# Block-by-block merge, output projection and second norm in a diffusion layer kernel, with gates fetched a channel tile ahead

## The chip, the cores and the metric

The kernel runs on one core of one Trainium2 chip. The time is device microseconds from start to end of one execution. In the text PE is TensorE, DVE is VectorE, ACT is ScalarE, POOL is GpSimd and SP is SyncE, whose queue issues every DMA of this kernel. "PEld" is the loading of weights into PE, which overlaps the matmuls.

## The reference

2048 latent positions of 1024 channels (and 256 context tokens) pass through a mixer and a gated convolutional MLP. The part that matters here lies between the two:

```python
def merge_branches(u, y_hgrn, w_a, w_b, w_out):
    y_a = fourier_mix(u[..., OFF_FNET:OFF_FNET + FNET_DIM]) @ w_a
    y_b = y_hgrn @ w_b
    g_a = jax.nn.sigmoid(u[..., OFF_GA:OFF_GB])
    g_b = jax.nn.sigmoid(u[..., OFF_GB:IN_DIM])
    return (g_a * y_a + g_b * y_b) @ w_out
...
x = x + mx[:, :, 2] * yx
h2 = modulate(rmsnorm(x, norm2_g[layer]), mx[:, :, 3], mx[:, :, 4])
x = x + mx[:, :, 5] * conv_ffn(h2, ...)
return rmsnorm(x, final_g)
```

Two branch outputs of 512 channels each are projected to 1024, multiplied by sigmoid gates and added, projected once more, added to x, and normed and modulated for the MLP.

## The kernel before

Every large product is made of three fp32r matmuls: each operand is split into a high part (ACT casts it, line 102) and a low part (raw minus high, line 103, on POOL or DVE), and hi·hi, hi·lo and lo·hi are added up in PSUM (`mm3`, lines 144 to 146). So every operand that comes from memory takes a DMA, a cast and a subtraction before PE can use it (`load_split`, line 105). The staging tile `rw` between the DMA and the subtraction has two buffers.

The program has three stages. `phase1` computes the input projections, the Fourier branch and the recurrence. Its last projections are the gates GA and GB: PE fills a PSUM bank, ACT evicts it into an `ev` tile of the pool `pe` (line 479), and SP stores that to memory (line 482). `phase2` is the stage of the change. `phase3` and `down` are the MLP.

`phase2` works on four blocks of 512 positions. For a block n there are three pieces of work:

- The merge (`branches`, line 855). Eight tiles `y`, four per branch, are loaded and split once. Then, for each of eight channel tiles j, a pair of weight tiles from w_a and w_b is loaded and split, PE makes 24 matmuls into two `pj` banks, DVE multiplies each by its gate tile (line 879), adds the two (line 881), and the sum is split into `mh` and `ml`. The two gate tiles are fetched in the same turn of the loop (line 876), into buffers of the pool `pe` that `phase1` used for evictions; there are three of them.
- The output projection (`out_proj`, line 886). For each of two halves c of the 1024 columns, 96 matmuls fill four banks, `wo`, under the tags `at` and `o` (two banks each). DVE multiplies them by `m2` and adds them to x (lines 912 and 913). The sums are stored to `dX` for the end of the layer (line 915).
- The second norm (`h2_block`, line 917). ACT sums the squares of the four x tiles (line 923), DVE computes the reciprocal root in a dozen tiny steps and scales x (line 928). The rest is a generator of eight steps (`modulate_steps`, line 419): four PE transposes into one bank (line 426), then an affine step on DVE (line 428), another on ACT (line 429) and a subtraction (line 431). These steps are called one at a time inside the loops of the next block, by `next(bg, None)`.

The order of the blocks before: merge 0, projection 0, merge 1 (with the steps of block 0), projection 1, merge 2 (with the steps of block 1), merge 3, projection 2, projection 3 (with the steps of block 2), and the steps of block 3 in the first matmuls of the MLP (`z`). A scheduler orders the instructions of each engine when the program is built; a pool's tile can only be filled when the tile that had its place has been read for the last time. Pools lie on a stack: `p4`, the pool of `phase2`, lies above `pe` while that one is open. The eight large places H0 to H7 are shared by tag: merges put `ml` and `mh` in H6 and H7, or in H4 and H5 for the last block.

Of the kernel before, what the change touches and what calls it, by code (L numbers as in the profile page):

```python
# [17 lines left out]
F32 = mybir.dt.float32  # L18
F32R = mybir.dt.float32r
# [7 lines left out]
P = 128  # L27
D = 1024
SEQ = 2048
CTX = 256  # L30
NB = 4
TB = 512
# [62 lines left out]
class Layer:  # L95
# [54 lines left out]
    def run(self):  # L150
        tc, nc = self.tc, self.nc
        with ExitStack() as es:
# [11 lines left out]
            with tc.tile_pool(name="pe", bufs=1, reuse_waits="tile") as self.pe:  # L164
                self.phase1()
                self.phase2()
# [252 lines left out]
    def modulate_steps(self, pool, xs, A, B, hi, lo, tags, every):  # L419

        nc = self.nc
        n = len(xs)
        for k in range(KD):
            pt = self.ps.tile([P, TB], F32, name="pt", tag=tags[k % len(tags)])
            for i in range(n):
                nc.tensor.transpose(pt[:, i * P:(i + 1) * P], xs[i][:, k * P:(k + 1) * P], self.eye)
            tmp = pool.tile([P, TB], F32, name="mt", tag="mt", bufs=2)
            nc.vector.tensor_scalar(tmp[:, :n * P], pt[:, :n * P], A[:, k:k + 1], B[:, k:k + 1], op0=MUL, op1=ADD)
            nc.scalar.activation(hi[:, k, :], pt[:, :n * P], AF.Identity, scale=A[:, k:k + 1], bias=B[:, k:k + 1])
            eng = nc.vector if k % every == every - 1 else nc.gpsimd  # L430
            eng.tensor_tensor(lo[:, k, :], tmp[:, :n * P], hi[:, k, :], op=SUB)
            yield
# [398 lines left out]
    def phase2(self):  # L831
        tc, nc, a, ps = self.tc, self.nc, self.a, self.ps
        self.h2 = [[None, None] for _ in range(NB)]
        with tc.tile_pool(name="p4", bufs=1, reuse_waits="tile") as p4:
            mg, bg = {}, iter(())
            for n in (0, 1):
                mg[n] = self.branches(p4, n, "H6", "H7", bg)
                x1 = self.ph.tile([P, 4, D], F32, name=f"x1{n}", tag=f"H{4 + n}")
                xs = [x1[:, i, :] for i in range(4)]
                self.out_proj(p4, n, mg[n], xs, bg)  # L840
                bg = self.h2_block(p4, n, xs, (2 * n, 2 * n + 1), ("tp", "at", "o"))
            mg[2] = self.branches(p4, 2, "H6", "H7", bg)
            mg[3] = self.branches(p4, 3, "H4", "H5", bg)
            for n in (2, 3):
                xs = [p4.tile([P, D], F32, name=f"x1{n}{i}", tag="yo", bufs=10) for i in range(4)]
                self.out_proj(p4, n, mg[n], xs, bg)
# [4 lines left out]
                bg = self.h2_block(p4, n, xs, ((6, 7), (4, 5))[n - 2], ("tp", "pj"))  # L851
# [3 lines left out]
    def branches(self, p4, n, t_lo, t_hi, bg):  # L855

        nc, a, ps = self.nc, self.a, self.ps
        mg_lo = self.ph.tile([P, KD, TB], F32R, name=f"ml{n}", tag=t_lo)
        mg_hi = self.ph.tile([P, KD, TB], F32R, name=f"mh{n}", tag=t_hi)
        br = []  # L860
        for b in range(2):
            for k in range(4):
                y = p4.tile([P, 2, TB], F32R, name=f"y{n}{b}{k}", tag="yo", bufs=10)
                self.load_split(y[:, 0, :], y[:, 1, :],
                                self.dY[k][:, n * TB:(n + 1) * TB] if b == 0 else self.dO[k][n][:], nc.vector, p4)
                br.append((y[:, 0, :], y[:, 1, :]))
        for j in range(KD):
# [5 lines left out]
            gts = []  # L873
            for b in range(2):
                gt = self.pe.tile([P, TB], F32, name="gt", tag="ev", bufs=3)
                nc.sync.dma_start(gt, (self.dGA if b == 0 else self.dGB)[j][n])
# [3 lines left out]
                gts.append(gt)  # L880
            nc.vector.tensor_tensor(gts[0], gts[0], gts[1], op=ADD)
            self.split(mg_hi[:, j, :], mg_lo[:, j, :], gts[0], nc.vector)
            next(bg, None)
        return mg_hi, mg_lo

    def out_proj(self, p4, n, mg, xs, bg):
# [6 lines left out]
        for c in range(2):  # L893
# [3 lines left out]
            accs = [ps.tile([P, TB], F32, name=f"wo{i}", tag="at" if i < 2 else "o") for i in range(4)]  # L897
            for k in range(KD):
# [10 lines left out]
                next(bg, None)  # L909
# [7 lines left out]
    def h2_block(self, p4, n, xs, slots, tags):  # L917
# [8 lines left out]
        rs = self.rsqrt(p4, vv, 4)  # L926
        for i in range(4):
            nc.vector.tensor_scalar(xs[i], xs[i], rs[:, i:i + 1], None, op0=MUL)
        self.h2[n] = [self.ph.tile([P, KD, TB], F32R, name=f"h2{n}{i}", tag=f"H{slots[i]}") for i in range(2)]
        return self.modulate_steps(p4, xs, self.mod2_A, self.mod2_B, *self.h2[n], tags, 4)  # L930
# [160 lines left out]
```

## Time and profile before

| what | value |
|---|---|
| time, median of 3 runs | 3182.1 us (3172.17 to 3186.12) |
| the profiled execution itself | 3175.0 us |
| its span, first to last instruction | 3173.2 us |
| matmuls and transposes on PE | 14955 |
| DVE busy | 1735.2 us |
| ACT busy | 930.4 us |
| POOL busy | 947.3 us |
| bytes moved | 372.59 MB |

The span is what the page's shares refer to; 1.8 us lie around it. PE's busy time counts overlapping matmuls once. "idle before" in the lists of groups is the time in which the engine did nothing just before an instruction of that group, with the instruction that ended the wait.

### The profile page before, as it was taken

How to read it: one execution, taken by the hardware profiler on the slowest of the kernel's cores; microseconds unless marked ns; L12 is line 12 of the kernel's file. 1: busy time of each engine (PE TensorE's matmuls, PEld its weight loads, DVE VectorE, ACT ScalarE, POOL GpSimd, SP SyncE). 2: the span in 40 equal slices, each digit the busy share in tenths (PEclk: the TensorE clock that was granted, in tenths of full speed). 3: DMA queues.
4: the chain of work that ended last, by engine and by line, in shares of the span. 5: the costliest groups of instructions: out<-in, count | busy, mean ns of one | idle time of the engine just before them, and what ended most of it. 6: DMA issues, size and time to landing. Idle time of an engine off the chain costs nothing.

```text
span 3173.2 us, 38929 instructions
## 1 busy us (share of the span) xinstructions
PE 3086.0 (97%) x14955; PEld 2554.0 (80%) x14955; DVE 1735.2 (55%) x2489; ACT 930.4 (29%) x1498; POOL 947.3 (30%) x563
## 2 busy tenths in 40 slices
PE   7999999999999999999999999999999998999998
PEld 4977788888888888777777888888888887788886
DVE  5355534566666640356645777777777777111324
ACT  4322211233333331233333232222222223223322
POOL 2200110000000010343532443444443445444443
PEclk9999999999999999999999999999999999999999
DMA  6255645423223322655642111111111113535643
GB/s 236 80 169 175 194 153 162 141 95 115 93 91 108 106 93 84 212 167 173 193 162 70 60 50 47 53 50 51 53 34 53 53 47 105 183 125 176 205 146 133
DMA packets 278506, 372.59 MB, mean 117 GB/s; under 512 B 20253, under 2 KB 154289, under 8 KB 274993
## 3 DMA queue, kind: packets, MB, share of 16 engines
q1 hardware_dynamic: 278321, 370.11, 35.6%
q8 instruction: 118, 1.93, 0.2%
q14 instruction: 67, 0.55, 0.1%
HBM read 268.58 MB, written 101.45 MB: 117 GB/s over the span
## 4 chain that ended last, share of the span: by engine, by line
PE 77%; DMA 6%; DVE 5%; POOL 2%; issue 2%; ACT 2%; SPq 0%; DVEq 0%; ACTq 0%; POOLq 0%
PE z L146 9%; PE z L145 9%; PE z L144 9%; PE pj L146 8%; PE pj L144 8%; PE pj L145 8%; PE dn L1035 5%; PE dn L1033 5%; PE dn L1034 5%; PE pa L773 4%; DMA rw<-in_w_b_dram 1%; PE kv L645 1%; PE wo L906 1%; PE wo L908 1%; PE wo L907 1%
## 5 line engine op out<-in xcount | busy, mean ns | idle before, releaser
L983 DVE SCALAR_TENSOR_TENSOR ac<-z,cw,ac 128x1953 f32<-128x1953 f32 (+2 forms) x308 | 700.8, 2275 | 255.4 <-ACT be L955 244.1
L144 PE MATMUL z<-h,w_up 128*128 128x512 f32 x1408 | 548.0, 389 | 1.9 <-ACT w_up L102 1.9
L146 PE MATMUL z<-h,w_up 128*128 128x512 f32 x1408 | 548.0, 389 | 0.0
L145 PE MATMUL z<-h,w_up 128*128 128x512 f32 x1408 | 548.0, 389 | 0.0
L959 POOL TENSOR_TENSOR ac<-ac,be 128x1984 f32<-128x1984 f32 x44 | 196.7, 4471 | 427.6 <-DVE ac L983 427.6
L103 POOL TENSOR_TENSOR gl<-rw,gh 128x512 fp32r<-128x512 f32 x176 | 233.0, 1326 | 271.7 <-ACT gh L102 262.2
L144 PEld LDWEIGHTS z<-h,w_up 128*128 128x128 f32 x1408 | 264.4, 188 | 57.0 <-ACT w_up L102 2.3
L145 PEld LDWEIGHTS z<-h,w_up 128*128 128x128 f32 x1408 | 264.4, 188 | 54.8
L146 PEld LDWEIGHTS z<-h,w_up 128*128 128x128 f32 x1408 | 264.4, 188 | 54.5
L1033 PE MATMUL dn<-wd,gh 128*128 128x512 f32 x704 | 279.0, 396 | 6.1 <-ACT gh L102 6.1
L1035 PE MATMUL dn<-wd,gl 128*128 128x512 f32 x704 | 279.2, 397 | 5.6 <-POOL gl L103 5.5
L1034 PE MATMUL dn<-wd,gh 128*128 128x512 f32 x704 | 278.6, 396 | 0.0
L953 ACT ACTIVATE ac<-z,vt,cw 128x2048 f32<-128x2048 f32 x44 | 90.9, 2066 | 639.0 <-PE z L146 639.0
L102 ACT CAST gh<-rw 128x512 fp32r<-128x512 f32 x176 | 108.6, 619 | 308.6 <-PE dn L1034 219.4
L479 ACT ACTIVATE ev<-pj 128x512 f32<-128x512 f32 (+1 forms) x136 | 79.6, 586 | 358.3 <-PE pj L146 336.9
L1035 PEld LDWEIGHTS dn<-wd,gl 128*128 128x128 f32 x704 | 133.3, 189 | 39.1 <-POOL gl L103 8.5
L1033 PEld LDWEIGHTS dn<-wd,gh 128*128 128x128 f32 x704 | 133.4, 189 | 37.6 <-ACT gh L102 7.0
L1051 DVE TENSOR_TENSOR dtmp<-dn,m 128x512 f32<-128x512 f32 x32 | 21.4, 684 | 251.6 <-PE dn L1035 251.5
L1034 PEld LDWEIGHTS dn<-wd,gh 128*128 128x128 f32 x704 | 133.3, 189 | 30.6
L103 POOL TENSOR_TENSOR w_up<-rw,w_up 128x512 fp32r<-128x512 f32 x88 | 112.8, 1306 | 92.0 <-ACT w_up L102 92.0
L773 PEld LDWEIGHTS pa<-bQ,bkc 128*128 128x128 f32 x896 | 120.7, 191 | 17.0 <-issue 10.5
L773 PE MATMUL pa<-bQ,bkc 128*128 128x128 f32 x896 | 127.5, 286 | 1.3
(304 smaller groups left out, 6185.6 us busy)
## 6 DMA issues: line engine op xcount, KB each, us to landing
rw<-dZ SPq DMA_DIRECT2D x176, 256.0 KB, 3.0
rw<-in_ffn_up_dram SPq DMA_DIRECT2D x88, 256.0 KB, 3.4
dZ<-ac SPq DMA_DIRECT2D x22, 1024.0 KB, 4.4
rw<-in_w_in_dram SPq DMA_DIRECT2D x80, 256.0 KB, 3.1
maw<-in_ada_w_dram SPq DMA_DIRECT2D x64, 256.0 KB, 3.1
rw<-in_w_out_dram SPq DMA_DIRECT2D x64, 256.0 KB, 2.6
x<-dX SPq DMA_DIRECT2D x48, 256.0 KB, 5.1
rw<-in_ffn_down_dram SPq DMA_DIRECT2D x44, 256.0 KB, 3.1
```

The source lines that it names most:

```text
L102: self.nc.scalar.copy(hi, raw)
L103: (eng or self.nc.gpsimd).tensor_tensor(lo, raw, hi, op=SUB)
L144: self.nc.tensor.matmul(ps, lh, rh, start=start and i == 0, stop=False)
L145: self.nc.tensor.matmul(ps, lh, rl, start=False, stop=False)
L146: mm = self.nc.tensor.matmul(ps, ll, rh, start=False, stop=stop and i == last)
L773: mm = nc.tensor.matmul(pa[:, c], kc[:, c], fap(Q, w * P, [(2 * m, nw), (W + m, 2), (1, m)]), start=True, stop=True)
L953: nc.scalar.activation(ac, z, AF.Identity, scale=self.cw[:, 4, jj:jj + 1], bias=self.v("cb", jj))
L959: nc.gpsimd.tensor_tensor(ac[:, :SEQ - 64], ac[:, :SEQ - 64], be[:, 64:], op=ADD)
L983: nc.vector.scalar_tensor_tensor(o, z3[:, r0 + dy:r1 + dy, c0 + dx:c1 + dx], self.cw[:, k, jj:jj + 1], o, op0=MUL, op1=ADD)
L1033: nc.tensor.matmul(accs[i], gh[:, t], wh, start=(kk == 0), stop=False)
L1034: nc.tensor.matmul(accs[i], gh[:, t], wl, start=False, stop=False)
L1035: nc.tensor.matmul(accs[i], gl[:, t], wh, start=False, stop=(kk == NF - 1))
```

## The change

The four blocks now go one after the other: merge n, projection n, second norm n, for n from 0 to 3. A merge fetches the gates of channel tile j + 1 before it works on tile j, from four buffers of its own in `p4`; the pool `pe` is closed before `phase2` opens `p4`, so that `p4` lies where `pe` lay. The `y` tiles have 8 places and not 10. The second column half of a projection uses the banks `pj` and `tp`; the first keeps `at` and `o`. The norm steps of a block are called from the second channel tile of the next merge on, with one more at that merge's end, and none inside a projection. Block 2's x goes where block 0's was (H4), which merge 3 needs for `ml`; so block 2's steps read x back from `dX`, four small pieces for each step (`reload_steps`), and scale them there.

```diff
@@ run
             with tc.tile_pool(name="pe", bufs=1, reuse_waits="tile") as self.pe:
                 self.phase1()
-                self.phase2()
+            self.phase2()
...
@@ modulate_steps
-    def modulate_steps(self, pool, xs, A, B, hi, lo, tags, every):
+    def modulate_steps(self, pool, xs, A, B, hi, lo, tags, every, k0=0, nk=KD):
...
-        for k in range(KD):
+        for k in range(k0, k0 + nk):
...
-                nc.tensor.transpose(pt[:, i * P:(i + 1) * P], xs[i][:, k * P:(k + 1) * P], self.eye)
+                nc.tensor.transpose(pt[:, i * P:(i + 1) * P], xs[i][:, (k - k0) * P:(k - k0 + 1) * P], self.eye)
...
@@ phase2
-            mg, bg = {}, iter(())
-            for n in (0, 1):
-                mg[n] = self.branches(p4, n, "H6", "H7", bg)
-                x1 = self.ph.tile([P, 4, D], F32, name=f"x1{n}", tag=f"H{4 + n}")
-                xs = [x1[:, i, :] for i in range(4)]
-                self.out_proj(p4, n, mg[n], xs, bg)
-                bg = self.h2_block(p4, n, xs, (2 * n, 2 * n + 1), ("tp", "at", "o"))
-            mg[2] = self.branches(p4, 2, "H6", "H7", bg)
-            mg[3] = self.branches(p4, 3, "H4", "H5", bg)
-            for n in (2, 3):
-                xs = [p4.tile([P, D], F32, name=f"x1{n}{i}", tag="yo", bufs=10) for i in range(4)]
-                self.out_proj(p4, n, mg[n], xs, bg)
+            bg = iter(())
+            for n in range(NB):
+                mg = self.branches(p4, n, *(("H6", "H7") if n < 3 else ("H4", "H5")), bg)
+                if n < 3:
+                    x1 = self.ph.tile([P, 4, D], F32, name=f"x1{n}", tag=f"H{4 + n % 2}")
+                    xs = [x1[:, i, :] for i in range(4)]
+                else:
+                    xs = [p4.tile([P, D], F32, name=f"x1{n}{i}", tag="yo", bufs=8) for i in range(4)]
+                self.out_proj(p4, n, mg, xs)
                 if n == 3:
...
-                bg = self.h2_block(p4, n, xs, ((6, 7), (4, 5))[n - 2], ("tp", "pj"))
+                bg = self.h2_block(p4, n, xs, ((0, 1), (2, 3), (6, 7), (4, 5))[n], ("tp", "at", "o") if n < 3 else ("tp", "pj"))
...
@@ branches
-        br = []
+        br, gates = [], {}
+
+        def load_gates(j):
+            gates[j] = [p4.tile([P, TB], F32, name=f"gt{b}", tag="gt", bufs=4) for b in range(2)]
+            for b in range(2):
+                nc.sync.dma_start(gates[j][b], (self.dGA if b == 0 else self.dGB)[j][n])
+
...
-                y = p4.tile([P, 2, TB], F32R, name=f"y{n}{b}{k}", tag="yo", bufs=10)
+                y = p4.tile([P, 2, TB], F32R, name=f"y{n}{b}{k}", tag="yo", bufs=8)
...
+        load_gates(0)
         for j in range(KD):
...
-            gts = []
+            if j + 1 < KD:
+                load_gates(j + 1)
+            gts = gates.pop(j)
             for b in range(2):
-                gt = self.pe.tile([P, TB], F32, name="gt", tag="ev", bufs=3)
-                nc.sync.dma_start(gt, (self.dGA if b == 0 else self.dGB)[j][n])
+                gt = gts[b]
...
-                gts.append(gt)
             nc.vector.tensor_tensor(gts[0], gts[0], gts[1], op=ADD)
             self.split(mg_hi[:, j, :], mg_lo[:, j, :], gts[0], nc.vector)
-            next(bg, None)
+            if j:
+                next(bg, None)
+        next(bg, None)
         return mg_hi, mg_lo
...
@@ out_proj
-            accs = [ps.tile([P, TB], F32, name=f"wo{i}", tag="at" if i < 2 else "o") for i in range(4)]
+            accs = [ps.tile([P, TB], F32, name=f"wo{i}", tag=("at", "at", "o", "o")[i] if c == 0 else ("pj", "pj", "tp", "tp")[i])
+                    for i in range(4)]
...
-                next(bg, None)
...
@@ h2_block
         rs = self.rsqrt(p4, vv, 4)
+        hi, lo = self.h2[n] = [self.ph.tile([P, KD, TB], F32R, name=f"h2{n}{i}", tag=f"H{slots[i]}") for i in range(2)]
+        if n == 2:
+            return self.reload_steps(p4, rs, hi, lo, tags)
         for i in range(4):
             nc.vector.tensor_scalar(xs[i], xs[i], rs[:, i:i + 1], None, op0=MUL)
-        self.h2[n] = [self.ph.tile([P, KD, TB], F32R, name=f"h2{n}{i}", tag=f"H{slots[i]}") for i in range(2)]
-        return self.modulate_steps(p4, xs, self.mod2_A, self.mod2_B, *self.h2[n], tags, 4)
+        return self.modulate_steps(p4, xs, self.mod2_A, self.mod2_B, hi, lo, tags, 4)
+
+    def reload_steps(self, p4, rs, hi, lo, tags):
+
+        nc = self.nc
+        for k in range(KD):
+            xc = p4.tile([P, 4, P], F32, name="xc", tag="xc", bufs=2)
+            for i in range(4):
+                nc.sync.dma_start(xc[:, i, :], self.dX[8 + i][:, k * P:(k + 1) * P])
+            nc.vector.tensor_tensor(xc, xc, fap(rs, 0, [(1, 4), (0, P)]), op=MUL)
+            xs = [xc[:, i, :] for i in range(4)]
+            yield from self.modulate_steps(p4, xs, self.mod2_A, self.mod2_B, hi, lo, tags, 4, k, 1)
```

The first place where the order moves is the start of the merges, on the queue of SP. Before, the loads of block 0's `y` (from `dY` and `dO`) stand among the stores of an earlier gate projection:

```order
L482 DMA dGA_0_191<-ev 128x512
L114 DMA rw<-dY_235 128x512
L114 DMA rw<-dY_236 128x512
L896 DMA m_11381<-dm_314 128x512
L114 DMA rw<-dY_237 128x512
L482 DMA dGA_1_192<-ev 128x512
L114 DMA rw<-dY_238 128x512
L114 DMA rw<-dO_0_239 128x512
L114 DMA rw<-dO_0_243 128x512
L482 DMA dGA_2_193<-ev 128x512
L114 DMA rw<-dO_0_247 128x512
L114 DMA rw<-dO_0_251 128x512
```

Now they stand behind the store of the last gate tile:

```order
L483 DMA dGB_3_234<-ev 128x512
L114 DMA rw<-in_w_a_dram 128x4x128
L114 DMA rw<-in_w_b_dram 128x4x128
L901 DMA x_11377<-in_x_dram 128x1024
L114 DMA rw<-dY_235 128x512
L114 DMA rw<-dY_236 128x512
L864 DMA gt_11025<-dGA_0_171 128x512
L864 DMA gt_11026<-dGB_0_203 128x512
L864 DMA gt_11038<-dGA_0_175 128x512
L114 DMA rw<-dY_237 128x512
L114 DMA rw<-dY_238 128x512
L864 DMA gt_11039<-dGB_0_207 128x512
```

Twenty-three more stores of gate tiles now stand ahead of the first load of `y` (in a name such as dGB_3_234 the 3 is the block and the last number a running one), and the loads of the first gates and of x stand between the loads of `y`.

On PE, at the same place, the matmuls of the first channel tile (weights `wab_11029`) all stood ahead of those of the second; now the second's (`wab_11073`) are put between them:

```order
L146 MATMUL pj_11042<-y003_11000,wab_11029 128x512
L144 MATMUL pj_11056<-y010_11005,wab_11029 128x512
L144 MATMUL pj_11086<-y000_10985,wab_11073 128x512
L145 MATMUL pj_11086<-y000_10985,wab_11073 128x512
L146 MATMUL pj_11086<-y000_10985,wab_11073 128x512
L145 MATMUL pj_11056<-y010_11005,wab_11029 128x512
L146 MATMUL pj_11056<-y010_11005,wab_11029 128x512
L144 MATMUL pj_11056<-y011_11010,wab_11029 128x512
L145 MATMUL pj_11056<-y011_11010,wab_11029 128x512
L146 MATMUL pj_11056<-y011_11010,wab_11029 128x512
L144 MATMUL pj_11086<-y001_10990,wab_11073 128x512
L145 MATMUL pj_11086<-y001_10990,wab_11073 128x512
```

Each `y` (the name has block, branch and index) is used for both channel tiles where it comes in; after the last one, y013, stand 11 of the 48 matmuls behind the one that takes its low part.

The second place is SP after a projection. Before, behind block 1's stores of x:

```order
L915 DMA dX_259<-x_12181 128x1024
L915 DMA dX_260<-x_12181 128x1024
L915 DMA dX_261<-x_12181 128x1024
L915 DMA dX_262<-x_12181 128x1024
L114 DMA rw<-in_w_a_dram 128x4x128
L876 DMA gt<-dGB_2_209 128x512
L114 DMA rw<-in_w_b_dram 128x4x128
L876 DMA gt<-dGA_2_181 128x512
L896 DMA m_13388<-dm_314 128x512
```

Now, behind block 2's stores, with the reloads `xc` of the first norm step:

```order
L924 DMA dX_263<-x_12987 128x1024
L924 DMA dX_264<-x_12987 128x1024
L924 DMA dX_265<-x_12987 128x1024
L924 DMA dX_266<-x_12987 128x1024
L949 DMA xc<-dX_263 128x128
L949 DMA xc<-dX_264 128x128
L864 DMA gt_13421<-dGA_3_182 128x512
L949 DMA xc<-dX_265 128x128
L949 DMA xc<-dX_266 128x128
L864 DMA gt_13422<-dGB_3_214 128x512
L114 DMA rw<-in_w_a_dram 128x4x128
```

The weights of the third channel tile (`in_w_a`, `in_w_b`) have moved from directly behind the stores to behind four reloads of what these stores wrote and two gates.

The third place is PE in merge 1, where the steps of block 0 begin. Before:

```order
L146 MATMUL pj<-y_11752,wab 128x512
L426 MATMUL pt<-eye,x_11376 128x128 x2
L144 MATMUL pj<-y_11717,wab 128x512
L145 MATMUL pj<-y_11717,wab 128x512
L426 MATMUL pt<-eye,x_11376 128x128 x2
L146 MATMUL pj<-y_11717,wab 128x512
L144 MATMUL pj<-y_11722,wab 128x512
L426 MATMUL pt<-eye,x_11376 128x128 x2
L145 MATMUL pj<-y_11722,wab 128x512
L426 MATMUL pt<-eye,x_11376 128x128 x2
```

Now:

```order
L146 MATMUL pj<-y_11753,wab 128x512
L427 MATMUL pt<-eye,x_11377 128x128
L144 MATMUL pj<-y_11718,wab 128x512
L145 MATMUL pj<-y_11718,wab 128x512
L427 MATMUL pt<-eye,x_11377 128x128
L146 MATMUL pj<-y_11718,wab 128x512
L144 MATMUL pj<-y_11723,wab 128x512
L145 MATMUL pj<-y_11723,wab 128x512
L427 MATMUL pt<-eye,x_11377 128x128
L146 MATMUL pj<-y_11723,wab 128x512
L144 MATMUL pj<-y_11728,wab 128x512
L427 MATMUL pt<-eye,x_11377 128x128
```

Both begin behind the same 48 matmuls (two channel tiles); before, each scaled x tile served the transposes of two steps, and now of one.

More of the change, by code (lines that the diff above doesn't have):

```diff
@@ L879, in branches, with out_proj @@
                 nc.vector.tensor_tensor(gt, pj, gt, op=MUL)
-                gts.append(gt)
             nc.vector.tensor_tensor(gts[0], gts[0], gts[1], op=ADD)
             self.split(mg_hi[:, j, :], mg_lo[:, j, :], gts[0], nc.vector)
-            next(bg, None)
+            if j:
+                next(bg, None)
+        next(bg, None)
         return mg_hi, mg_lo
-    def out_proj(self, p4, n, mg, xs, bg):
+    def out_proj(self, p4, n, mg, xs):
         nc, a, ps = self.nc, self.a, self.ps
```

## The prediction

> **What bounds the kernel now.** I read the page first, for the share of PE, then the stage table for the stretch that the change touches, then the list of groups on PE there, because its last column tells what PE waited for.
>
> ```profile
> span 3173.2 us, 38929 instructions
> PE 3086.0 (97%) x14955; PEld 2554.0 (80%) x14955; DVE 1735.2 (55%) x2489; ACT 930.4 (29%) x1498; POOL 947.3 (30%) x563
> 1291.99:1690.17 398.18, 371.51 (x1634) 297.75 (x1633) 229.80 (x323) 139.16 (x233) 160.02 (x115) 0.99 0.56 180
> 1690.17:2665.00 974.83, 970.19 (x4292) 802.84 (x4292) 704.41 (x331) 272.17 (x223) 419.29 (x167) 1.00 0.16 52
> ```
>
> PE is busy 97% of the span, and in the MLP stage that follows (second row of the stage table, 970.19 of 974.83) it never rests. So a microsecond that PE gains or loses between 1292 and 1690 us moves the end by as much. That stretch lasts 398.18 us, and PE (first column of busy time) works in 371.51 of them: what the change can win is at most some 27 us, under 1%. The list of groups says who takes them:
>
> ```profile
> L144 PE MATMUL pj<-y,wab 128*128 128x512 f32 x256 | 102.5, 401 | 8.9 <-DVE gt L879 7.1 <-ACT y L102 1.3 <-ACT wab L102 0.4
> L145 PE MATMUL pj<-y,wab 128*128 128x512 f32 x256 | 100.9, 394 | 1.2 <-DVE y L103 1.2
> L906 PE MATMUL wo<-wo,mh 128*128 128x512 f32 x256 | 100.8, 395 | 7.2 <-DVE mt L912 5.9 <-ACT h L429 1.2
> L907 PE MATMUL wo<-wo,mh 128*128 128x512 f32 x256 | 100.0, 391 | 0.5 <-POOL wo L103 0.5
> L426 PE MATMUL pt<-eye,x 128*128 128x128 f32 x128 | 22.1, 291 | 8.9 <-DVE x L928 7.9 <-ACT h L429 1.1
> L144 PE MATMUL z<-h,w_up 128*128 128x512 f32 x27 | 10.8, 401 | 1.9 <-ACT w_up L102 1.9
> DVE gt L879 <- DMA gt<-dGB: 125.7, 15, 102.5
> ```
>
> Idle time behind the second bar sums to 28.6 us. The last row, of the waits, has the reason of the first: DVE waited 15 times for a gate tile to land, once for 102.5 us in which there was nothing to do, and 23.2 us otherwise.
>
> **What the change removes.** Five waits. The gate multiplications' 7.1 us: gates now come a tile early. I keep 1.5 of it, since SP still queues weights behind gates that wait for a buffer, so 5.6 go. The bank waits (mt L912) of 5.9: the second half has banks of its own. After it, the next merge wants these banks, but its first one is free when the projection's first accumulator is evicted, and
>
> ```profile
> 1382.59 1.37 DVE mt L912 x2
> 1384.21 0.39 PE L908 MATMUL wo<-wo,ml 128*128 128x512 f32 x1
> 1393.11 0.69 DVE L103 TENSOR_TENSOR ml<-gt,mh 128x512 fp32r<-128x512 f32 x1
> ```
>
> the first row (of the chain) has two evictions done at 1382.59 + 1.37 = 1383.96, before the projection's last matmul (second row, 1384.2); so nothing comes back there. If evictions were late, it would be the 1.2 us of one. The loads of y in merge 3 (1.3 and 1.2), as a projection lies between any two merges now. The start of z, 1.9: its four banks are those of the first half now, long empty; w_up was cast by then. And wo L907, 0.5. That is 5.6 + 5.9 + 2.5 + 1.9 + 0.5 = 16.4 us of idle time. A stop costs more than its idle time:
>
> ```profile
> 1313.75 0.39 PE L145 MATMUL pj<-y,wab 128*128 128x512 f32 x1
> 1313.97 0.39 PE L146 MATMUL pj<-y,wab 128*128 128x512 f32 x1
> 1315.21 0.47 PE L144 MATMUL pj<-y,wab 128*128 128x512 f32 x1 [0.85 <-DVE gt L879]
> ```
>
> Matmuls start 0.227 us apart (0.22 in the first two rows, 43.5 us for the 192 of a merge); the third starts 1.24 after the second, so 1.01 is lost with 0.85 idle, a factor of 1.2. So 16.4 becomes **20 us removed** (idle alone 16; with all of the gates' wait and the clock, 24).
>
> The norm steps' wait (x L928, 7.9) I leave in: in the order the first transposes stand behind the same 48 matmuls as before, and what they wait for, evictions, squares, root and scaling, is the same work in the same place. It was called one channel tile later, but not put later.
>
> **What it adds at the start.** The y of block 0 were loaded by 1200 us, among the gate projections. Now their loads stand on SP behind the last gate store and two weight loads that wait for POOL:
>
> ```profile
> 1292.91 0.33 SPq L482 DMA_DIRECT2D dGB<-ev  x1
> 1293.47 2.54 POOL L103 TENSOR_TENSOR wab<-rw,wab 128x512 fp32r<-128x512 f32 x2 [19.22 <-ACT wab L102]
> 1296.16 0.38 SPq L114 DMA_DIRECT2D rw<-in_w_b_dram  x1
> 1296.60 0.49 SPq L892 DMA_DIRECT2D x<-in_x_dram  x1
> ```
>
> So the first y is issued at 1297.1 and the second at 1297.5. How long one takes, the chain shows where a y was late before:
>
> ```profile
> 1338.29 4.25 DMA rw<-dO
> 1343.22 0.70 DVE y L103
> 1343.94 3.43 DMA rw<-dO
> 1348.05 0.70 DVE y L103
> 1348.77 4.19 DMA rw<-dY
> ```
>
> From one issue to the next, when a staging buffer is waited for, 5.65 and 4.83 us: landing, cast, subtraction. Two buffers take two y at a time, eight y are four rounds, so the last is ready at 1297.5 + 4 x 5.24 = 1318.5. Of the 48 matmuls of the first two channel tiles 11 stand behind it, 11 x 0.227 = 2.5: 1321.0. Before, 48 matmuls from 1292.04 took 10.9 and ended at 1302.9. **Loss 18 us** (all rounds of 4.83: 16.5; of 5.65: 20). Without the interleaving of two tiles it would be 3 more. Nothing covers it: there is no other matmul that is ready.
>
> The granted clock falls after a stop:
>
> ```profile
> 1498.33 0.69 PE L426 MATMUL pt<-eye,x 128*128 128x128 f32 x2 [3.05 <-DVE x L928]
> 1495.00:1500.00 5.00, 1.95 (x9) 1.37 (x7) 4.79 (x11) 1.16 (x2) 2.26 (x2) 0.82 0.63 197
> 1500.00:1505.00 5.00, 5.00 (x23) 4.08 (x22) 4.86 (x7) 2.13 (x4) 2.00 (x3) 0.84 0.29 73
> 1505.00:1510.00 5.00, 5.00 (x26) 4.13 (x25) 3.38 (x5) 2.65 (x5) 5.00 (x5) 1.00 0.41 137
> ```
>
> After 3.05 us of idling the means are 0.82 and 0.84, then 1.00: a missing (0.18 + 0.16) x 5 = 1.7 us of full clock. The start has a wait of 9 us and three of some 3, but most slow matmuls fall into later waits; I add **1 us**, bounds 0 and 3. [...]
>
> **What it adds in merge 3.** The third channel tile's weights were issued 5.2 us after projection 0's last matmul (1384.2; first row below). Now they stand behind reads of what the stores of x wrote, and behind a gate whose buffer is free when `ml` is written, in merge 1 at 1393.11 + 0.69 = 1393.8 (row above); `ml` waits itself for these stores to land. That is 9.6 us after the last matmul.
>
> ```profile
> 1389.37 0.38 SPq L114 DMA_DIRECT2D rw<-in_w_a_dram  x1
> rw<-in_w_a_dram SPq DMA_DIRECT2D x6, 256.0 KB, 3.2
> L102 ACT CAST wab<-rw x64: 610/620/627, 1271.0 to 1579.4; 128x512 fp32r<-128x512 f32 x64
> L103 POOL TENSOR_TENSOR wab<-rw,wab x64: 1261/1296/1831, 1271.7 to 1581.1; 128x512 fp32r<-128x512 f32 x64
> ```
>
> Four more issues of 0.38, 3.2 us to land, 0.62 to cast, 1.3 to subtract: 9.6 + 1.5 + 3.2 + 0.6 + 1.3 = 16.2, and PE needs the low part at 10.9 + 0.4 (transposes) + 0.5 = 11.8. So 4.4 us, and 1.7 for the clock: **6 us** (nothing, if SP is held up less than the two tiles of work that PE has; 10, if the next tile waits too). The 32 reloads and eight multiplications on DVE (0.7 each, against four of 1.2 before) are otherwise beside PE's 5.4 us per tile. The two norm steps that stand together at a merge's end cost about what the wait for h L429 (1.2) did.
>
> **The sum.** -20 + 18 + 1 + 6 = +5 us. The profiled execution took 3175.0 (span 3173.2 and 1.8 around it), 7 below the median of 3182.1; 0.5% of it, some 16 us, is about what a measurement of this kernel can tell from no change. From the median, 3187.
>
> **Rivals.**
>
> Weights for gates: PE waits no more for gates but for the weights, which SP issues between them. For: the channel tile's period was up to 6.9 us with gates late, and weights need 3.2 + 0.6 + 1.3 = 5.1 of 5.4. Against: only 0.4 us of wait stood at wab so far. Then the 5.6 x 1.2 stay: 3194.
>
> The reload in every step, the slower side. In merge 3 SP issues four reloads, two gates and two weights per channel tile, 8 x 0.38 = 3.0 us, and several wait for PE or DVE with all behind them. Weights are staged in two buffers; if their issue slips behind the previous tile's transposes by more than 5.4 + 0.4 - 5.1 = 0.7 us, each tile stops PE. Three us in seven tiles are 21: 3208. Against: from the fifth tile on, the weights stand ahead of that tile's gates.
>
> The change does more than I grant: the steps come late enough that x L928's 7.9 x 1.2 = 9.5 and two losses of clock (3.4) go, and the y come in rounds of 4.8. Then 5 - 13 - 2 = -10: 3172. For over 0.5% the reload must be free as well: 3166. Against it is the order.
>
> **How the numbers follow.** Forecast 0.55; weights for gates 0.20; reload in every step 0.15; does more 0.10. The bounds (16 to 24 removed, 16 to 23 at the start, 0 to 10 in merge 3) give -8 to +17, so 3174 to 3199; the range reaches to 3171 and 3205 for parts of the rivals. Faster by over 0.5% (below 3166) 0.06, slower (above 3198) 0.18, the rest 0.76.
>
> **What would show it.** A stop of PE of some 9 us at 1292, three shorter ones, and merge 1 some 13 us late by 1384; no waits of wo for mt L912; gates landing ahead of PE; a stop of 4 us behind the second channel tile of merge 3. Wrong would be: a y landing before 1292, transposes that do not wait, or PE waiting for wab in every tile of merge 3.

## The result and the profile after

| | before | changed kernel |
|---|---|---|
| median of 20 runs | 3176.9 us (3170.4 to 3186.6) | 3187.1 us (3183.8 to 3205.4) |
| ratio to before | | 1.0033, 95% interval 1.0025 to 1.0042 |
| profiled execution | 3175.0 us | 3185.2 us |

The changed kernel is slower by a third of a per cent, 10.2 us between the medians. The prediction was 3187 us, 5 more than before, too little to tell from no change. Part of the agreement is luck: over 20 runs the median of before is 3176.9 and not 3182.1, and the change cost 10 us where 5 were forecast. The two differences cancel. The loss is small, but with 20 runs of each its interval lies clear of 1; the 16 us that the prediction took for the least that can be told from no change was too much.

The page of the changed kernel, its first line and its row of busy times:

```profile
span 3183.4 us, 38973 instructions
PE 3091.7 (97%) x14955; PEld 2559.8 (80%) x14955; DVE 1738.4 (55%) x2493; ACT 931.5 (29%) x1498; POOL 945.6 (30%) x563
```

The stage tables follow, first of the changed kernel, then one row of before. The first row is the whole stretch from the end of the gate projections to the first matmul of z; the others are merge 0, projections 0, 1 and 2, and merge 3. The columns are the window, its length, the busy time of PE, PEld, DVE, ACT and POOL, PE's granted clock, the DMA share and GB/s.

```profile
1290.53:1699.13 408.60, 376.17 (x1633) 303.18 (x1633) 236.10 (x333) 144.70 (x241) 157.59 (x114) 0.96 0.58 188
1290.53:1358.58 68.05, 50.83 (x193) 38.06 (x193) 30.34 (x38) 19.98 (x34) 21.23 (x15) 0.87 0.65 213
1358.58:1403.08 44.50, 43.84 (x193) 35.96 (x192) 20.93 (x30) 13.80 (x23) 11.60 (x9) 1.00 0.51 164
...
1453.74:1501.10 47.36, 45.56 (x196) 37.18 (x194) 21.93 (x31) 14.48 (x25) 12.89 (x10) 0.96 0.61 194
...
1553.05:1598.78 45.73, 43.95 (x195) 36.06 (x194) 21.69 (x31) 14.48 (x25) 12.87 (x10) 1.00 0.45 145
1598.78:1653.82 55.04, 49.59 (x225) 39.87 (x224) 38.80 (x64) 22.29 (x37) 27.97 (x20) 0.97 0.74 228
```

```profile
1292.04:1339.56 47.52, 44.58 (x193) 35.72 (x192) 25.37 (x32) 15.01 (x26) 20.65 (x15) 1.00 0.73 238
```

The stretch took 408.60 us where it took 398.18: 10.4 more, the whole of the loss. PE idled 32.4 us of it (408.60 - 376.17) against 26.7, and was busy 376.2 against 371.5 for the same matmuls. So a good half of the loss is counted as idle time, and the rest as PE being busy longer at a lower clock (0.96 against 0.99); what the clock itself cost is worked out further down. Merge 0 alone lost 68.05 - 47.52 = 20.5 us. The rest of the stretch won 10 back.

The list of groups on PE, in the same window as the prediction's:

```profile
L144 PE MATMUL pj<-y,wab 128*128 128x512 f32 x256 | 104.9, 410 | 18.8 <-ACT y L102 14.5 <-DVE gt L886 2.6 <-ACT wab L102 1.7
L146 PE MATMUL pj<-y,wab 128*128 128x512 f32 x256 | 103.3, 404 | 0.4 <-POOL wab L103 0.4
L916 PE MATMUL wo<-wo,mh 128*128 128x512 f32 x256 | 101.2, 396 | 3.6 <-ACT h L430 3.6
L917 PE MATMUL wo<-wo,mh 128*128 128x512 f32 x256 | 100.9, 394 | 0.7 <-POOL wo L103 0.7
L427 PE MATMUL pt<-eye,x 128*128 128x128 f32 x85 | 14.2, 280 | 6.2 <-DVE x L940 6.2
L427 PE MATMUL pt<-eye,xc 128*128 128x128 f32 x32 | 4.9, 274 | 3.9 <-issue 2.4 <-DVE xc L950 1.4
```

The waits that the change was said to remove are gone: no bank waits for an eviction of the projection (5.9 before), no y is late in merge 3 (2.5), nothing stops the start of z (1.9), and the gates cost 2.6 in place of 7.1. What came in their place is in the same rows: 14.5 for y, 3.6 for h L430, 3.9 for xc, 1.7 for weights.

**The start.** SP's timeline, then PE's stops:

```profile
1291.39 0.33 SPq L483 DMA_DIRECT2D dGB<-ev  x1
1293.24 0.38 SPq L114 DMA_DIRECT2D rw<-in_w_a_dram  x1
1294.46 0.38 SPq L114 DMA_DIRECT2D rw<-in_w_b_dram  x1
1294.89 0.50 SPq L901 DMA_DIRECT2D x<-in_x_dram  x1
1295.44 0.90 SPq L114 DMA_DIRECT2D rw<-dY  x2
1302.66 1.01 SPq L114 DMA_DIRECT2D rw<-dY  x2
1306.92 1.87 SPq L114 DMA_DIRECT2D rw<-dO  x2
1312.57 1.40 SPq L114 DMA_DIRECT2D rw<-dO  x2
```

```profile
1301.96 0.80 PE L144 MATMUL pj<-y,wab 128*128 128x512 f32 x1 [11.27 <-ACT y L102]
1306.21 0.79 PE L144 MATMUL pj<-y,wab 128*128 128x512 f32 x1 [1.03 <-ACT y L102]
1311.87 0.73 PE L144 MATMUL pj<-y,wab 128*128 128x512 f32 x2 [2.15 <-ACT y L102]
1318.64 0.50 PE L144 MATMUL pj<-y,wab 128*128 128x512 f32 x1 [0.33 <-DVE gt L886]
```

The gate projections ended 1.5 us sooner here, so the forecast's 1297.1 for the first y means 1295.6; it was issued at 1295.44. The y came in four rounds, as forecast. From one issue to the next they took 7.2, 4.3 and 5.7 us, and the fourth took 6.6 to the end of its first subtraction, which stood on DVE behind a gate multiplication:

```profile
1317.89 0.69 DVE L886 TENSOR_TENSOR gt<-pj,gt 128x512 f32<-128x512 f32 x1 [4.29 <-PE pj L146]
1318.50 1.28 DVE L103 TENSOR_TENSOR y<-rw,y 128x512 fp32r<-128x512 f32 x2
```

The four stops of PE add up to 14.8 us of idle time, and PE was busy 6.25 us longer in merge 0 (50.83 against 44.58) for the same 192 matmuls.

**The ends of the merges.** PE at the start of projection 1, then in merge 3 (first row the transposes, second the weights of the third channel tile):

```profile
1459.23 0.50 PE L916 MATMUL wo<-wo,mh 128*128 128x512 f32 x1 [1.80 <-ACT h L430]
```

```profile
1611.26 0.65 PE L427 MATMUL pt<-eye,xc 128*128 128x128 f32 x4 [1.44 <-DVE xc L950]
1613.29 0.72 PE L144 MATMUL pj<-y,wab 128*128 128x512 f32 x1 [1.38 <-ACT wab L102]
...
1653.44 0.63 PE L427 MATMUL pt<-eye,xc 128*128 128x128 f32 x4 [2.43 <-issue]
```

Two norm steps put eight transposes at a merge's end with no matmul between them, and the projection begins behind them. It works on three of its four banks for 15 matmuls (3.3 us). The fourth is the one that the eighth step was given, and PE waits until ACT has read it (h L430). In merge 3 the scaling of the second step's x pieces came late (last row, for which the profile names no releaser). The pieces had landed by 1650.8, but DVE scaled them only from 1652.66 on, behind three other operations, the first of which had waited 2.75 us for the cast of a w_out piece.

### The profile page after: what moved, and what is told of

The parts are those of the page before. It is cut to its first block, busy times and chain, and to the rows that moved or that the text cites. A ratio compares the mean times of both kernels' runs of the same rounds, so it can differ in the third digit from the quotient of the medians.

```text
span 3183.4 us, 38973 instructions
## 1 busy us (share of the span) xinstructions
PE 3091.7 (97%) x14955; PEld 2559.8 (80%) x14955; DVE 1738.4 (55%) x2493; ACT 931.5 (29%) x1498; POOL 945.6 (30%) x563
## 4 chain that ended last, share of the span: by engine, by line
PE 82%; DMA 6%; DVE 4%; issue 3%; POOL 2%; ACT 2%; SPq 0%; ACTq 0%; DVEq 0%; POOLq 0%
PE z L146 9%; PE z L145 9%; PE z L144 9%; PE pj L144 9%; PE pj L146 9%; PE pj L145 9%; PE dn L1057 4%; PE dn L1055 4%; PE dn L1056 4%; PE pa L774 4%; DMA rw<-in_ffn_down_dram 1%; PE wo L916 1%; PE wo L918 1%; PE wo L917 1%; PE kv L646 1%
## 5 line engine op out<-in xcount | busy, mean ns | idle before, releaser
L774 PEld LDWEIGHTS pa<-bQ,bkc 128*128 128x128 f32 x896 | 120.6, 191 | 16.9 <-issue 10.4
L103 POOL TENSOR_TENSOR wab<-rw,wab 128x512 fp32r<-128x512 f32 x64 | 89.3, 1407 | 148.0 <-ACT wab L102 148.0
```

The costliest lines, as they stand in the source:

```text
L103: (eng or self.nc.gpsimd).tensor_tensor(lo, raw, hi, op=SUB)
L774: mm = nc.tensor.matmul(pa[:, c], kc[:, c], fap(Q, w * P, [(2 * m, nw), (W + m, 2), (1, m)]), start=True, stop=True)
```

## The experiments

All ratios are to the kernel before, from runs on the same chip. "Stretch" is the time from the end of the gate projections to the first matmul of z in the profiled execution. That is one execution: e2_last_step's is the longest of its seven runs, 3192.0 us with a median of 3183.2, so its stretch is long for its ratio.

| run | ratio (95% interval) | stretch, us |
|---|---|---|
| changed kernel | 1.0033 (1.0025 to 1.0042) | 408.6 |
| e1_early_y | 0.9956 (0.9944 to 0.9969) | 382.2 |
| h1_place | 0.9980 (0.9971 to 0.9989) | 392.6 |
| e2_last_step | 1.0021 (1.0008 to 1.0033) | 411.1 |
| e3_both | 0.9941 (0.9928 to 0.9955) | 381.8 |
| b1_banks | 0.9983 (0.9974 to 0.9992) | 396.2 |
| e5_gates_turn | 1.0019 (1.0010 to 1.0029) | 408.6 |
| e4_later | 0.9954 (0.9942 to 0.9967) | 383.5 |
| f1_act | 0.9944 (0.9932 to 0.9956) | 389.6 |
| f2_xlate | 0.9916 (0.9901 to 0.9930) | 376.2 |
| h2_best | 0.9954 (0.9942 to 0.9967) | 386.6 |
| h4_xhalf | 1.0010 (0.9999 to 1.0021) | 398.5 |
| g1_split | 0.9924 (0.9911 to 0.9938) | 378.2 |

### e1_early_y: the place of y

```diff
                 self.phase1()
-            self.phase2()
+                self.phase2()
...
-            gates[j] = [p4.tile(..., name=f"gt{b}", tag="gt", bufs=4) for b in range(2)]
+            gates[j] = [p4.tile(..., name="gt0", tag="gt", bufs=2), self.pe.tile(..., name="gt1", tag="ev", bufs=3)]
```

> The changed kernel with one thing undone: the pool pe stays open during phase 2, so the y tiles lie beside it and not in its place. GB's gate tiles use the three ev buffers, GA's two buffers in p4. Theory (place): block 0's y are loaded among the gate projections again, merge 0 takes some 48 us and not 68, the 11.4 us stop ahead of it and the three after it go: 20 us less, ratio to before about 0.997 (3167). Rival (queue): the y wait for the backlog of gate stores on SP whatever place they have: merge 0 still starts some 10 us late, 3187. Rival (three ev buffers for GB bring the gate waits back): 5 us of the 20 are lost again, 3172.

The ratio is 0.9956: 0.77% less than the changed kernel, 24 us, and faster than before. On SP the y stand among the gate projections again, as the first two of them show, and the group of merge matmuls has lost its wait for y:

```profile
1167.83 0.88 SPq L114 DMA_DIRECT2D rw<-dY  x2
```

```profile
L144 PE MATMUL pj<-y,wab 128*128 128x512 f32 x256 | 102.4, 400 | 3.7 <-DVE gt L886 3.6
```

Merge 0 took 48.3 us, as the theory of the place has it, and the rival of the queue is out. The waits for gates (3.6) stayed a microsecond above the changed kernel's 2.6, not the five of the third theory. Merge 3 became shorter too, 50.96 us for 55.04, which nobody expected. So this run alone does not say whether the place or the other gate buffers did it.

### h1_place: the place alone

```diff
-        with tc.tile_pool(name="p4", ...) as p4:
+        with tc.tile_pool(name="pg", ...) as self.pg, tc.tile_pool(name="p4", ...) as p4:
...
-            gates[j] = [p4.tile(...
+            gates[j] = [self.pg.tile(...
```

> The changed kernel with one line more: the four gate buffers in a pool of their own, opened ahead of p4, so that they lie where the pool pe lay and the y tiles above it; pe stays closed, the gates keep four buffers. Theory (place): what held block 0's y back was only the place; they load among the gate projections, the start's 20 us go, 0.997 of before. In e1_early_y 4 us more went in merge 3 with other gate buffers; if that was due to the buffers, merge 3 stays near 55 us here. Rival: pe being closed ahead of phase 2 is what holds the y back, wherever they lie: merge 0 starts 11 us late again, 1.003.

The y load early, merge 0 starts without a stop, and 17 us of the 24 go (0.9980). The start's loss was due to the place. But the place that `pe` leaves late still holds something: now the first gates, which SP issues from 1295.74 on, and for which DVE, and PE behind it, waits once:

```profile
1302.51 0.77 PE L144 MATMUL pj<-y,wab 128*128 128x512 f32 x1 [6.14 <-DVE gt L886]
```

Merge 3 took 55.86 us, as in the changed kernel. The place did not shorten it, which leaves the gate buffers. In the changed kernel and here both gates of a tile share four places, and the gate ahead of the third tile's weights on SP waits for one of them; in e1_early_y, GA and GB have places of their own, five in all, and w_a goes out first, 6.8 us after the merge's start in place of 10.5:

```profile
1608.90 0.32 SPq L864 DMA_DIRECT2D gt<-dGB  x1
1609.26 0.43 SPq L114 DMA_DIRECT2D rw<-in_w_a_dram  x1
```

```profile
1585.03 0.38 SPq L114 DMA_DIRECT2D rw<-in_w_a_dram  x1
```

(The first two rows are of the changed kernel, whose merge 3 starts at 1598.78; the last is of e1_early_y, whose merge 3 starts at 1578.21.)

### e2_last_step and e3_both: two steps at a merge's end

```diff
                 next(bg, None)
-        next(bg, None)
         return mg_hi, mg_lo
...
                     nc.tensor.matmul(accs[i], mg_lo[:, k, t], hi[:, q, :], ...)
+                if c == 1 and k == 0:
+                    next(bg, None)
```

> The changed kernel with the eighth norm step moved from a merge's end to behind the first 12 matmuls of the next projection's second half. Theory (two steps together): the stops behind h L430 at the start of projections 1 and 2 (lost 1.96 and 1.94, and 1.6 of clock after the first) and the one of 2.48 ahead of projection 3 (and 1.6 of clock) were due to two steps standing together; they go, 8 to 10 us less, 3178. Rival (evictions): ACT and DVE have the same work at that place, and PE waits for the sixth step's eviction at the same bank: 3185 to 3187. Merge 0 stays at 68 us.

> Both edits, the early y and the eighth step in the projection. Theory: the two losses are in different places and add up: 20 + 9 = 29 us less than the changed kernel, 3158, and faster than before by 0.6%. Rival: what is won at the start comes back as later stops in merge 1 to 3 (SP queue): 3165 or more.

Projections 1 and 2 took 44.14 us each in both runs, where they took 47.36 and 45.73 in the changed kernel, and no matmul of a projection waits for h L430. So the stops there were due to the two steps. Yet the time fell by 0.12% and, from e1_early_y to e3_both, by 0.15%: 4 to 5 us, half of what was expected. The intervals overlap, so in the time the gain is not shown. In the profiles most of what was won came back at one place, the start of projection 3, which took 49.3 us in e3_both and 44.8 in e1_early_y. Its SP and PE rows in e3_both:

```profile
1622.89 2.92 SPq L900 DMA_DIRECT2D x<-in_x_dram  x4
1625.90 2.16 SPq L114 DMA_DIRECT2D rw<-in_w_out_dram  x2
```

```profile
1634.32 0.49 PE L915 MATMUL wo<-wo,mh 128*128 128x512 f32 x1 [2.09 <-ACT wo L102]
```

Four loads of x (512 KB each, wanted only at the half's end) stood ahead of the third and fourth piece of w_out. ACT cast these pieces at 1633.65, 7.8 us after SP issued the first.

### f2_xlate: x behind the weights

```diff
-        for i in range(4):
-            r0 = n * TB + i * P
-            nc.sync.dma_start(xs[i], a["x"][0, r0:r0 + P, :])
...
                 self.load_split(hi[:, q, :], lo[:, q, :], a["w_out"][...], ...)
+                if c == 0 and k > 3:
+                    r0 = n * TB + (k - 4) * P
+                    nc.sync.dma_start(xs[k - 4], a["x"][0, r0:r0 + P, :])
```

This is e3_both and the edit shown.

> As e3_both, and a projection's four loads of x are written among the weights of its first half and not ahead of them; on SP they move only in projection 3, where four x (512 KB each) stood ahead of the third and fourth piece of w_out. Theory (transfer): those pieces landed some 5 us after their issue because they shared the DMA engines with the x; PE lost 2.3, 1.1 and 2 of clock at the start of projection 3; most of it goes, projection 3 takes 45 and not 49.3 us, 0.993 of before. Rival (queue of staging buffers): the pieces are late since the staging buffers come free late, whatever stands ahead: projection 3 stays at 49, 0.994.

Projection 3 took 44.3 us, and the ratio is 0.9916: 27 us faster than before at the medians, and the lowest ratio of the study (four of its six runs took 3151 to 3155 us, two some 3163; g1_split's interval overlaps with it). In its rows the first x stands behind the first two pieces of w_out, and the projections wait for nothing:

```profile
1616.17 1.57 SPq L114 DMA_DIRECT2D rw<-in_w_out_dram  x2
...
1618.80 0.38 SPq L912 DMA_DIRECT2D x<-in_x_dram  x1
1621.72 0.33 SPq L114 DMA_DIRECT2D rw<-in_w_out_dram  x1
```

```profile
L915 PE MATMUL wo<-wo,mh 128*128 128x512 f32 x256 | 100.3, 392 | 0.0
L427 PE MATMUL pt<-eye,x 128*128 128x128 f32 x96 | 16.1, 280 | 8.2 <-DVE x L941 7.2 <-ACT h L430 1.0
```

What is left is mostly the norm's own chain, x L941.

### b1_banks: the banks alone, in the kernel before

```diff
-            accs = [ps.tile(..., tag="at" if i < 2 else "o") for i in range(4)]
+            accs = [ps.tile(..., tag=("at", "at", "o", "o")[i] if c == 0 or n > 2 else ("pj", "pj", "tp", "tp")[i]) for i in range(4)]
```

> The kernel before with one part of the change: in projections 0 to 2 the second column half takes the banks pj and tp. Theory (banks): the stops behind mt L912 there (lost 0.50 and 0.62, 0.47 and 0.62, 1.34 and 0.63, together 4.2 us) go and nothing comes back; those of projection 3 (1.72 and 1.22) stay; 4 us less, about 0.999 of before, to be read from the list of groups more than from the time. Rival (the banks bite later): the next merge's first matmuls wait for the evictions from pj, and merges 1 and 2 get as much longer.

The ratio is 0.9983, some 5 us less, where 4 were expected. The bank waits in the projections fell from 5.9 to 0.9, which is projection 3's:

```profile
L906 PE MATMUL wo<-wo,mh 128*128 128x512 f32 x256 | 100.6, 393 | 4.3 <-ACT h L429 1.7 <-ACT wo L102 1.7 <-DVE mt L912 0.9
```

Projections 0 and 1 are 1.2 and 0.9 us shorter, 2 and 3 together 2.1: the 4.2 of the theory. Merge 1, and merges 2 and 3 together, stand within 0.6 us of before, so nothing came back there. (Merge 0, where the two kernels do the same, was 2.2 us longer in this profile.)

### e5_gates_turn: gates not a tile ahead

```diff
-        load_gates(0)
...
-            if j + 1 < KD:
-                load_gates(j + 1)
+            load_gates(j)
```

> The changed kernel with the gates of a channel tile fetched in its own turn again, from the same four buffers. Theory (ahead): the fetch a tile ahead is what took the waits for gates away; without it they come back as DVE waiting for dGA and dGB to land and PE behind it, some 5 us more, 3192. Rival (buffers): four buffers of their own let the loads run ahead in any case; within 2 us of the changed kernel, 3187.

The ratio is 1.0019; the fetch a tile ahead brought nothing that can be measured. The gate multiplications on DVE, in the changed kernel and then in e5_gates_turn:

```profile
L886 DVE TENSOR_TENSOR gt<-pj,gt 128x512 f32<-128x512 f32 x64 | 43.4, 683 | 25.2 <-PE pj L146 23.3 <-DMA gt<-dGA 1.4 <-DMA gt<-dGB 0.5
```

```profile
L884 DVE TENSOR_TENSOR gt<-pj,gt 128x512 f32<-128x512 f32 x64 | 43.6, 684 | 24.5 <-PE pj L146 21.6 <-DMA gt<-dGA 2.6 <-DMA gt<-dGB 0.2
```

Before, DVE waited 23.2 us for gates to land (and once 102.5 with nothing to do); here it is 1.9 and 2.8. The fetch a tile ahead is not the reason, since the loads landed early without it too. The gates' own four buffers are the likely one; no run tested them alone.

### e4_later, f1_act, g1_split: the norm's chain

e4_later is e1_early_y with the steps called from the third channel tile on (`if j > 1`) and the last two in the projection's second half; the steps also take their banks in another order (`at`, `o`, `tp`). f1_act scales x on ACT besides; g1_split is f2_xlate with two of the four scalings on ACT. The edit of f1_act:

```diff
-            nc.vector.tensor_scalar(xs[i], xs[i], rs[:, i:i + 1], None, op0=MUL)
+            nc.scalar.activation(xs[i], xs[i], AF.Identity, scale=rs[:, i:i + 1])
```

> As with both edits, and the norm steps start one channel tile later still: the first transposes of a block stand behind 72 matmuls of the next merge and not 48, the seventh and eighth step behind 12 and 24 matmuls of the projection's second half. Theory (too early, x L940): the transposes waited because the scaled x is ready some 12 to 14 us after the projection; behind 72 matmuls (16.3 us) nothing waits, some 3.6, 4.3 and, with the third tile's weights in merge 3, 3 to 5 us go: 3147. Rival (DVE's work just moves): DVE is as late with the next tile's gates, PE stops there: 3158.

> As e4_later, and the scaling of x by the reciprocal root on ACT and not on DVE. Theory (DVE in order): with the transposes late enough, PE stopped in merges 1 and 2 since the four scalings (3.75 us on DVE) stand ahead of the second tile's gate multiplications, which free the pj banks; without them the stops of 2.74 and 4.01 and 1.6 and 2.4 of clock go: 8 to 10 us less than e4_later, 0.993 of before. Rival (ACT in order): four scalings of 1.04 on ACT hold up the casts of the next tile's weights, and PE waits for wab L102 there as long: 0.995.

> As f2_xlate, and two of a block's four scalings of x on ACT, two on DVE. Theory (chain): in f2_xlate the transposes of merges 1 and 2 still stopped PE (lost 2.66, 3.78 and 1.6 of clock) at the end of a chain of evictions, squares, root and four scalings on DVE (0.94 each); two at once on two engines end it 1.9 us sooner: 4 to 5 us less, 0.990 of before. Rival (as in f1_act): the stop goes from the transposes to the casts of the next weights, which ACT makes after the scalings: no better than f2_xlate, 0.9916.

In all three nothing was gained, as the rival had it, but its reason was right only in e4_later. There, with the transposes behind 72 matmuls, their wait for x goes (1.1 us left, in z). But PE then stops 9.5 us for gates, where e1_early_y has 3.6, and 2.6 for a cast of weights. In merge 2 DVE does the four scalings in one piece, and the gate multiplication that frees PE's bank stands behind them:

```profile
1495.74 3.75 DVE L941 TENSOR_SCALAR x<-x,rs_y 128x1024 f32<-128x1024 f32 x4
1499.41 0.68 DVE L886 TENSOR_TENSOR gt<-pj,gt 128x512 f32<-128x512 f32 x1
```

With the scalings on ACT (f1_act), PE waited 1.4 for casts of weights, not more as the rival had it but less, and still 8.9 for gates and 2.1 for the root. With two on each (g1_split) it did not wait for casts at all, but 7.0 for x where f2_xlate has 7.2. In merge 1 the two scalings on ACT took 2.19 us, where DVE had needed 2.74 for all four in f2_xlate, and from the last addition to x to the end of the root it took 0.8 us longer: nothing was won. What would shorten this chain was not found.

### h2_best and h4_xhalf: two misses

h2_best is h1_place with the edits of f2_xlate. h4_xhalf also loads x and takes its squares by column half; POOL writes a column of each place first, which holds a load back until a weight piece has been cast.

> As h1_place, with the eighth step in the projection and x written among the weights (the edits of f2_xlate on other gate buffers). Theory: 0.9916 as f2_xlate, and 2 to 4 us less, since merge 0's 4.6 us behind gates were due to three shared buffers for GB. Rival: those stops come from the late cast of mh behind late weights, and four buffers change nothing: 0.9916.

> As h2_best, with x loaded by column half, each piece behind a weight piece of its projection (POOL writes one column of the place first, which the load then waits for), and the squares taken by column half in the projection (ACT, eight of 512 and one addition on DVE in place of four of 1024). Theory: merge 0's stops go with the eight x loads (512 KB each) that stood among its weights, 4 us; the second half's squares take half the time ahead of the root, so the transposes' stops (2.66, 3.78 and 1.6 of clock in f2_xlate) shrink by 2 us each: 8 us less than h2_best, 0.989 of before. Rival: the x pieces now compete with w_out's and the next y, and PE stops in the projections: no better than h2_best.

h2_best stands at 0.9954, 12 us above f2_xlate. Merge 0 took 53.6 us for 48.5 and merge 3 52.7 for 49.8, the same two places at which h1_place was behind e1_early_y; merge 1 was longer too, by 2.5 us. So the gate buffers of e1_early_y (three and two, with `pe` left open) are better than four shared ones in a pool of their own. Whether it is that they are separate, or five, or where they lie, no run tells. In h4_xhalf merge 0 fell to 48.3 us even so, as expected, but each projection grew to 47 to 49:

```profile
L917 PE MATMUL wo<-wo,mh 128*128 128x512 f32 x256 | 101.9, 398 | 6.7 <-POOL wo L103 6.6
```

POOL makes the low parts of w_out's pieces, and what was added to its queue there held them up. The edit changes three things, so how much is POOL and how much the x pieces in the DMA queue stays open. No run took the x loads out of merge 0 alone.

## Why the prediction was right, and where it was not

**Bound.** Right: the other stages kept their time, and the whole loss lies in the stretch of phase 2.

**What goes.** Forecast 16.4 us of idle time, measured 14.6 (7.1 - 2.6 of gates, 5.9, 2.5, 1.9, and 0.2 more behind wo). The banks were confirmed by b1_banks. The gates' share was 4.5 where 5.6 was forecast, and the reason given was wrong: not the fetch ahead, as e5_gates_turn showed, but most likely the buffers. That the 2.5 of y and the 1.9 of z went because of the new order of the blocks is read from the traces; no run tested the order alone.

**The start.** Forecast a loss of 18 and 1 for the clock; measured 20.5 for merge 0, and 20.8 already at the end of its first 48 matmuls (32.1 us into the stretch, where before it was 11.3). The mechanism was the forecast one, to 0.2 us in the time of the first issue, and e1_early_y and h1_place show it to be the place. What was too small is the term of the rounds: 23.8 us for the four, where 4 x 5.24 = 21.0 were taken. These 2.8 us are what the loss has over the 18. The clock did fall:

```profile
1300.00:1305.00 5.00, 3.04 (x6) 1.78 (x6) 1.38 (x2) 1.24 (x2) 0.00 (x0) 0.50 0.72 254
1305.00:1310.00 5.00, 3.69 (x7) 1.58 (x6) 1.63 (x3) 1.24 (x2) 0.00 (x0) 0.54 0.92 303
```

But "most slow matmuls fall into later waits" held. PE reached the first y of the fourth round at 1317.81, just as its cast ended (1317.76), and once the last low part was there (1319.79) the rest ran at full pace (granted clock 1.00 from 1316.44 on). So nearly all of the 6.25 us for which PE was busy longer stand where it would have waited. At most the 0.69 us of the gate multiplication at 1317.89, which waited for PE and held up the last subtractions, can be the clock's, so the 1 us taken was enough.

**Merge 3.** Forecast 6 us; PE idled 1.44 + 1.38 + 0.21 there, 3.0 us, and ran its next matmuls at half pace (granted clock 0.50 from 1613.40 to 1616.81). The gate and the weights went out 10.1 and 10.5 us after the merge's start (forecast 9.6 and the issues behind it). The mechanism, the shared gate buffers, is what h1_place and e1_early_y separate.

**The two steps at a merge's end.** This is the step that failed. The prediction let them "cost about what the wait for h L429 (1.2) did", that is nothing more than before. They cost 3.6 us of idle behind h L430 and 2.4 ahead of projection 3, 4.8 more than before, and the clock twice (0.50 for 3.41 us from 1459.80, and again from 1654.36). For the first projection affected, the row 1453.74:1501.10 has a clock of 0.96 where that of projection 0 has 1.00. e2_last_step and e3_both took the stops in projections 1 and 2 away, and the one ahead of projection 3, where PE then waited for w_out.

**The transposes' wait.** Left in, and right: 6.2 after, 7.9 before.

In idle time the terms are -14.6 removed, +14.5 for y, +3.1 in merge 3 (1.4, 1.3 and 0.4), +4.8 for the two steps, -1.7 for the transposes: 6.1, and PE was busy 4.7 us longer. That gives 10.8 against the 10.4 measured. The forecast +5 missed the two steps, with their two falls of the clock, and the longer rounds of y. Of its rivals none came: PE does not wait for weights in every tile, the reload hurts in one tile and at the merge's end, and the transposes still wait.

## What to carry to other kernels

Closing a pool before opening the next puts the first tiles of the next stage in places that are freed last; ask which loads go there, and give those places to the tile that is needed latest. A wait that is spread out (one step per tile) should not be gathered at a stage's end, where the next stage wants the same banks at once. When a stop goes and the time does not, look for the next late arrival on the DMA queue: here four loads that were not yet needed stood ahead of two that were, and writing them a few lines later took projection 3 from 49.3 to 44.3 us.

## What the runs showed of the hardware

The clock also fell after short stops, and not after all of them. After the 1.80 us at 1459.23 the next five microseconds had a mean of 0.68, while in projection 2, after a stop of 1.78 in the same place, the row 1553.05:1598.78 has a clock of 1.00.

```profile
1460.00:1465.00 5.00, 5.00 (x16) 3.93 (x16) 1.31 (x3) 1.67 (x3) 1.15 (x1) 0.68 0.88 269
```

In the traces of the kernel before and of the changed kernel, between 1280 and 1720 us, the granted clock is 1.00 or 0.50, and each time at 0.50 lasted 3.41 us, but for the first in the changed kernel, which lasted 13.65 (from 1295.96 to 1309.62). Counted in stretches of 3.41 us that begin and end where the clock changed, the two traces have 8 at full clock that were followed by one at half clock. PE idled 1.80 to 3.41 us in each of these, in one stop or in several. In the 236 that were followed by full clock it idled 1.87 at most. From half clock, the 8 stretches followed by full clock had at most 0.25 us of idling, and the 3 followed by half clock 1.02 to 3.41. Each of the two stops above lies whole in one stretch, where the two groups meet. The stop of 1.92 ahead of z in the kernel before (it ended at 1690.17) fell into two stretches with 1.06 and 0.85 us of idling, and the clock stayed at 1.00. In the half-clock stretch from 1459.80 matmuls started 0.43 us apart, behind it 0.23. A stretch of busy PE at half clock loses 1.7 us (3.41 x 0.50). Outside the start, the changed kernel has four at half clock (from 1459.80, 1514.42, 1613.40 and 1654.36), the kernel before two (from 1399.18 and 1498.16).

The tiny steps of the root on DVE (128x4 elements) took 0.15 to 0.17 us in e4_later, in the chain from 1490.14 to 1495.71, wherever POOL was idle. Two of them began 0.03 and 0.01 us behind a subtraction on POOL and took 1.28 and 1.31 us; they ended 0.02 and 0.03 us after it. The first, DVE and POOL:

```profile
1492.50 1.28 DVE L126 SCALAR_TENSOR_TENSOR rs_t<-rs_t,vv 128x4 f32<-128x4 f32 x1
```

```profile
1492.47 1.29 POOL L103 TENSOR_TENSOR wab<-rw,wab 128x512 fp32r<-128x512 f32 x1 [4.96 <-ACT wab L102]
```

The second, of 1.31 us, fell beside POOL's next subtraction (1494.00, 1.29 us). The two lengthen the chain that the transposes wait for by 2.3 us. What held them up was not tested in any run.
